# Three of the seven PSUM sums of each down product go to an adding transfer instead of VectorE

## The chip, the cores and the metric

The kernel runs on one core of a Trainium2 chip. Its time is the device time of one launch in microseconds (us), and runs are compared by their medians. Beside the timed runs there is one profiled execution, whose trace gives all durations below.

## The reference

A two-layer decoder trunk in float32 on x of 1024 tokens by 1024 features. Layer 0 is latent attention (low-rank queries and keys/values, rotary keys) and a SwiGLU feed-forward; layer 1 is differential attention over keys and values made from layer 0's result, and again a feed-forward. What the change touches is the second half of the feed-forward, the product with `w_down` and the residual:

```python
D_FF = 2816
def _swiglu(h, w_gate_up, w_down):
    gu = h @ w_gate_up
    return (jax.nn.silu(gu[..., :D_FF]) * gu[..., D_FF:]) @ w_down
...
    h = h + _swiglu(_rmsnorm(h, ffn_norm[l]), ffn_w_gate_up[l], ffn_w_down[l])
return _rmsnorm(h, final_norm)
```

## The kernel before, in words

Everything is stored transposed: features on the 128 partitions, 512 tokens (half a sequence) in a row of a tile. Each float32 operand is split into a high and a low part; a product is three matmuls (high by high, high by low, low by high). ScalarE makes the high part by a copy, VectorE or GpSimd the low part by a subtraction. So a weight `wr` becomes `wh` and `wl`, and an activation `stg` becomes `xh` and `xl`.

The feed-forward of a layer is `block_tail`. Its down product is done by Strassen's scheme in Winograd's form: 2 by 2 blocks, seven products instead of eight. The 2816 inner features are 22 tiles of 128, paired into 11; the pairs are worked off in four groups of 2, 3, 3 and 3 (`GROUPS`). For the first three groups and each of four output blocks n = 0..3, `down(g, n, xs)` runs products 0 to 6. A product has three matmuls for each pair of its group, so 6 matmuls in the first group and 9 in the next two. The last group is done by `down_last`, which the change leaves alone.

The seven products of a block gather in three PSUM banks: `a` (products 0, 2, 4, 6, on top of each other), `b` (product 1) and `c` (products 3 and 5). After each product the bank as it then stands is added into one of four state tiles `h11, h12, h21, h22` in SBUF, which hold the residual and all groups' sums. Before the change each of these seven adds is `add(t, ps)`, a VectorE tensor_tensor that reads the bank and the state tile and writes the state tile. A product that goes on in the same bank has to wait until the bank has been read: product 5 for the sum of product 3, product 6 for the sum of product 4. `h22` gets the sums of products 3 and 4, `h12` of 2 and 5, `h11` of 0 and 1, `h21` of 6.

Beside this, VectorE makes the block differences of the weights (`wr<-wr`), their low parts (`wl`), the sums of the activations of the next group (`stg<-stg`), and part of their low parts (`xl`); GpSimd does the other `xl`. Weights come by SP's DMA queue into eight buffers `wr`, made by `raw()`.

The order of instructions is not that of the code. `Plan` records all operations of a stage, gives each a cost (`cost`: duration on its engine, and delay until another engine can use the result), and replays them by a list schedule: on each engine the operation that can start first. It also decides which buffer a tile gets. The engines then run their queues in that order, so a wait at the head of a queue holds up all behind it. In the trace every operation has line 287, that of the replay, and is told apart by its tiles.

Of the kernel before, what the change touches and what calls it, by code (L numbers as in the profile page):

```python
# [14 lines left out]
AF = mybir.ActivationFunctionType  # L15
ALU = mybir.AluOpType
# [176 lines left out]
class Plan:  # L193
# [100 lines left out]
    def cost(self, engine, name, n, dtype, psum, accum, size):  # L294

        if engine == "tensor":
            if name == "transpose":
                return 0.107, self.HOP
            return n * (1 if dtype == F32R else 6 if n <= 64 else 8) / 2400, self.HOP
        if engine == "scalar":  # L300
            return (0.05 if psum else 0.09) + n / 1200 + 0.19 * accum, self.HOP
        if engine == "vector":
            return 0.067 + n / 960 + 0.063 * (name == "scalar_tensor_tensor" and not psum), self.HOP
        if engine == "gpsimd":
            return (0.245 + n / 1200 if name == "tensor_scalar" else 0.15 + n / 475), self.HOP
        return max(0.45, size / 360e3), 2.2
# [64 lines left out]
def trunk(ctx: ExitStack, tc: tile.TileContext, A: dict):  # L371
    nc = Plan(tc)
# [28 lines left out]
    def bank(name="ps"):  # L401
        if nc.on:
            return nc.ask(banks[0], [P, HF], F32, name, banks[1].get(name))
        return mm.tile([P, HF], F32, name=name, tag="mm")
# [137 lines left out]
    with tc.using_default_side("right"):  # L542
# [9 lines left out]
                t=("z6", "z7", "z8", "z9", "t", "t"), xh=[q + "h" for q in spare], xl=[q + "l" for q in spare],  # L552
# [76 lines left out]
    for k in range(KT):  # L629
        xt[k] = load_x(0, k)  # L630
        raw = wa_p.tile([P, NA * P], F32, name="war", tag="war", bufs=3)
# [434 lines left out]
    def block_tail(layer, half, resid, last, side_work=None, ahead=None, meanwhile=None):  # L1066
# [17 lines left out]
        def htile(n, f, name="h"):  # L1084
            return hp.tile([P, HF], F32, name=name, tag=f"h{n}{f}")
# [11 lines left out]
        def raw(src=None, np_=4):  # L1097
            t = wp.tile([P, HF], F32, name="wr", tag="wr", bufs=8)
            if src is not None:
                nc.sync.dma_start(out=t[:, : np_ * P], in_=src)  # L1100
            return t

        def acc_a():
            return mm2.tile([P, HF], F32, name="pa", tag="pa")

        def acc_c(name="pc"):
            return mm2.tile([P, HF], F32, name=name, tag="pc", bufs=2)
# [90 lines left out]
        def product(ps, i, cols, xs, start=True):  # L1198
            wh, wl = cols.get(i)
            n = len(xs[i])  # L1200
            for k, (xh, xl) in enumerate(xs[i]):
                c = slice(k * P, (k + 1) * P)
                nc.tensor.matmul(ps, lhsT=wh[:, c], rhs=xh, start=start and k == 0, stop=False, skip_group_check=not start)
                nc.tensor.matmul(ps, lhsT=wh[:, c], rhs=xl, start=False, stop=False, skip_group_check=not start)
                nc.tensor.matmul(ps, lhsT=wl[:, c], rhs=xh, start=False, stop=k == n - 1, skip_group_check=not start)
# [127 lines left out]
        def wd(g, n, *how):  # L1333
            p0, np_ = GROUPS[g][0], len(GROUPS[g])
            return Columns([A["wd"][layer, n, :, b, p0 : p0 + np_, :].rearrange("p k c -> p (k c)") for b in range(4)], np_, *how)

        def add(t, ps):
            nc.vector.tensor_tensor(t, t, ps, ALU.add)

        def down(g, n, xs):  # L1340

            cols = wd(g, n)
            if g == 0:
                for f in range(2):
                    for m in (n, n + 4):
                        h[f][m] = htile(m, f)
                        nc.sync.dma_start(out=h[f][m], in_=h_mid[f, m])
            h11, h12, h21, h22 = h[0][n], h[0][n + 4], h[1][n], h[1][n + 4]
            a = acc_a()
            product(a, 0, cols, xs)  # L1350
            add(h11, a)
            yield
            b = bank("pb")
            product(b, 1, cols, xs)
            add(h11, b)
            yield
            product(a, 2, cols, xs, start=False)
            add(h12, a)
            yield
            c = acc_c()  # L1360
            product(c, 3, cols, xs)
            add(h22, c)
            yield
            product(a, 4, cols, xs, start=False)
            add(h22, a)
            yield
            product(c, 5, cols, xs, start=False)
            add(h12, c)
            yield
            product(a, 6, cols, xs, start=False)  # L1370
            add(h21, a)
            yield
# [137 lines left out]
        for i, src in ((5, h[0][4:]), (6, h[1][4:])):  # L1510
            for k in range(4):
                x[i][k] = xtile(i, k)
                c = L if k < 2 else slice(0, HF)
# [31 lines left out]
        for g in range(len(GROUPS) - 1):  # L1545
            after = [[] for _ in range(7)]
            taken = [SLOTS[p] for p in GROUPS[g]]
            free = [p for p in GROUPS[g + 1] if SLOTS[p] not in taken]
            more = [p for p in GROUPS[g + 1] if p not in free]
            side = prepare(after, free, more)  # L1550
            for n in range(4):
                i = 0
                for _ in down(g, n, xs):
                    next(side, None)
                    if n == 3:
                        for p in more:
                            place(after, p, i)
                    i += 1
            xs = after
# [101 lines left out]
    def last0(f, h, r, tmp, _=None):  # L1661
# [18 lines left out]
        low()  # L1680

    block_tail(0, half0, A["x"], last0, positions_and_lambda, ahead0, lambda: both(0)).close()


# [162 lines left out]
    def last1(f, h, r, tmp, c=slice(0, HF)):  # L1847
        for k in range(KT):
# [3 lines left out]
            yield  # L1852

    block_tail(1, half1, h_spill, last1).close()


# [58 lines left out]
```

## Time and profile before

| what | us |
|---|---|
| median of 3 timed runs | 2554.65 (2553.1 to 2556.36) |
| the profiled execution, whole | 2557.78 |
| its span, first to last instruction | 2555.9 |
| mean granted TensorE clock | 0.973 |

The busy time of the engines over the span is PE 2350.6 us, VectorE (DVE) 1992.9, ScalarE (ACT) 1167.8 and GpSimd (POOL) 1063.3. The first three groups of the down product run from about 1010 to 1172 us in layer 0 and from about 2308 to 2470 us in layer 1. A share over the whole span says little about these two stretches; the windows further down are cut there.

### The profile page before, as it was taken

How to read it: one execution, taken by the hardware profiler on the slowest of the kernel's cores; microseconds unless marked ns; L12 is line 12 of the kernel's file. 1: busy time of each engine (PE TensorE's matmuls, PEld its weight loads, DVE VectorE, ACT ScalarE, POOL GpSimd, SP SyncE). 2: the span in 40 equal slices, each digit the busy share in tenths (PEclk: the TensorE clock that was granted, in tenths of full speed). 3: DMA queues.
4: the chain of work that ended last, by engine and by line, in shares of the span. 5: the costliest groups of instructions: out<-in, count | busy, mean ns of one | idle time of the engine just before them, and what ended most of it. 6: DMA issues, size and time to landing. Idle time of an engine off the chain costs nothing. (4 is left out here: it accounts for less than half of the span.)

```text
span 2555.9 us, 37477 instructions
## 1 busy us (share of the span) xinstructions
PE 2350.6 (92%) x12744; PEld 2001.0 (78%) x12744; DVE 1992.9 (78%) x3743; ACT 1167.8 (46%) x2319; POOL 1063.3 (42%) x921
## 2 busy tenths in 40 slices
PE   8699999978899998899999999999879999988997
PEld 6579988757688886777788898888657888876777
DVE  6475555399987879999767667675799887889997
ACT  4145545245344445344345555453444444454442
POOL 2132222176555554123344445443467555543212
PEclk9899999999999999999999999999899999999999
DMA  5132234622322225332233323463612222235322
GB/s 180 21 128 63 67 109 146 179 72 85 116 79 83 85 81 186 105 105 91 76 109 105 110 90 115 140 217 104 185 42 86 89 83 75 91 113 168 108 72 73
DMA packets 162351, 270.29 MB, mean 106 GB/s; under 512 B 22128, under 2 KB 55152, under 8 KB 162160
## 3 DMA queue, kind: packets, MB, share of 16 engines
q1 hardware_dynamic: 162160, 267.90, 34.2%
q8 instruction: 101, 1.65, 0.3%
q14 instruction: 90, 0.74, 0.1%
HBM read 197.43 MB, written 61.49 MB: 101 GB/s over the span
## 5 line engine op out<-in xcount | busy, mean ns | idle before, releaser
L287 ACT ACTIVATE wh<-wr 128x512 fp32r<-128x512 f32 (+2 forms) x588 | 322.2, 557 | 489.1 <-PE pb L287 128.0
L287 DVE TENSOR_TENSOR wl<-wr,wh 128x512 fp32r<-128x512 f32 (+2 forms) x588 | 451.8, 782 | 41.9 <-ACT wh L287 39.7
L287 PE MATMUL pa<-xh,wh 128*128 128x512 f32 (+1 forms) x850 | 342.1, 403 | 38.7 <-DVE h L287 15.9
L287 PE MATMUL pa<-xh,wl 128*128 128x512 f32 (+1 forms) x850 | 339.2, 400 | 19.2 <-DVE wl L287 18.5
L287 PE MATMUL pa<-xl,wh 128*128 128x512 f32 (+1 forms) x850 | 338.7, 399 | 7.1 <-DVE xl L287 7.1
L287 POOL TENSOR_TENSOR wr<-wr 128x512 f32<-128x512 f32 x176 | 250.2, 1426 | 207.2 <-DMA wr<-wgu 99.3
L287 PE MATMUL pb<-xh,wh 128*128 128x256 f32 (+1 forms) x976 | 293.8, 304 | 25.5 <-DVE s L287 19.7
L287 PE MATMUL pb<-xh,wl 128*128 128x256 f32 (+1 forms) x976 | 291.6, 301 | 2.4 <-DVE wl L287 2.2
L287 PE MATMUL pb<-xl,wh 128*128 128x256 f32 (+1 forms) x976 | 292.4, 301 | 1.5 <-DVE xl L287 1.5
L287 POOL TENSOR_TENSOR xl<-stg,xh 128x512 fp32r<-128x512 f32 x66 | 111.0, 1700 | 303.4 <-ACT xh L287 162.9
L287 PEld LDWEIGHTS pa<-xh,wh 128*128 128x128 f32 x850 | 163.1, 192 | 83.4 <-DVE h L287 15.8
L287 PEld LDWEIGHTS pb<-xh,wh 128*128 128x128 f32 x976 | 186.5, 192 | 51.8 <-DVE s L287 30.2
L287 POOL TENSOR_SCALAR p<-p,tot 128x640 f32<-128x640 f32 (+7 forms) x128 | 98.3, 769 | 272.9 <-DVE tot L287 194.7
L287 PEld LDWEIGHTS pa<-xh,wl 128*128 128x128 f32 x850 | 163.8, 193 | 59.9 <-DVE wl L287 28.5
L287 PEld LDWEIGHTS pb<-xl,wh 128*128 128x128 f32 x976 | 187.6, 192 | 15.1 <-DVE xl L287 2.3
L287 PEld LDWEIGHTS pb<-xh,wl 128*128 128x128 f32 x976 | 187.1, 192 | 10.1 <-DVE wl L287 4.4
L287 PEld LDWEIGHTS pa<-xl,wh 128*128 128x128 f32 x850 | 164.2, 193 | 38.7 <-DVE xl L287 9.4
L287 ACT ACTIVATE p<-sc,nmax 128x128 f32<-128x128 f32 (+7 forms) x192 | 141.9, 741 | 78.7 <-DVE nmax L287 53.4
L287 PE MATMUL pc<-xl,wh 128*128 128x512 f32 x352 | 139.8, 397 | 9.9 <-DVE xl L287 9.9
L287 POOL TENSOR_TENSOR qt<-wr 128x256 f32<-128x256 f32 x120 | 105.8, 901 | 98.4 <-DVE wl L287 80.6
L287 PE MATMUL pc<-xh,wh 128*128 128x512 f32 x352 | 138.7, 396 | 8.6 <-DVE h L287 7.8
L287 PE MATMUL pc<-xh,wl 128*128 128x512 f32 x352 | 139.3, 396 | 1.6 <-DVE wl L287 1.6
(288 smaller groups left out, 6310.7 us busy)
## 6 DMA issues: line engine op xcount, KB each, us to landing
wr<-wgu SPq DMA_DIRECT2D x176, 256.0 KB, 3.2
act_d<-s SPq DMA_DIRECT2D x88, 256.0 KB, 2.5
stg<-act_d SPq DMA_DIRECT2D x88, 256.0 KB, 2.8
wr<-wd SPq DMA_DIRECT2D x96, 192.0 KB, 2.4
wr<-wo SPq DMA_DIRECT2D x56, 256.0 KB, 3.9
h<-h_mid SPq DMA_DIRECT2D x48, 256.0 KB, 4.5
h_mid<-h SPq DMA_DIRECT2D x32, 256.0 KB, 2.2
oh<-o_hi SPq DMA_DIRECT2D x28, 256.0 KB, 5.1
```

Of the source, the lines that this page charges most:

```text
L287: return getattr(getattr(self.nc, engine), name)(*map(put, args), **{k: put(a) for k, a in kw.items()})
```

## The change

A new helper `pour(t, ps)` takes the place of `add` for products 1, 3 and 5 of `down`: ScalarE copies the bank into a `wr` buffer, and a DMA issued by GpSimd adds that buffer into the state tile (`accum_op=ALU.add`). The sums of products 0, 2, 4 and 6 stay on VectorE. With three groups, four blocks and three sums that is 36 pours in a layer and 72 in all. `Plan.cost` learns a cost for such a DMA, which only the schedule uses.

```diff
@@ cost
         if engine == "vector":
             return 0.067 + n / 960 + 0.063 * (name == "scalar_tensor_tensor" and not psum), self.HOP
+        if name == "dma_start" and engine == "gpsimd":
+            return 1.2, 3.0
         if engine == "gpsimd":
@@ block_tail
         def add(t, ps):
             nc.vector.tensor_tensor(t, t, ps, ALU.add)
 
+        def pour(t, ps):
+
+            e = raw()
+            nc.scalar.activation(e, ps, AF.Copy)
+            nc.gpsimd.dma_start(out=t, in_=e, accum_op=ALU.add)
+
@@ down
             product(b, 1, cols, xs)
-            add(h11, b)
+            pour(h11, b)
             yield
             product(a, 2, cols, xs, start=False)
             add(h12, a)
             yield
             c = acc_c()
             product(c, 3, cols, xs)
-            add(h22, c)
+            pour(h22, c)
             yield
             product(a, 4, cols, xs, start=False)
             add(h22, a)
             yield
             product(c, 5, cols, xs, start=False)
-            add(h12, c)
+            pour(h12, c)
             yield
             product(a, 6, cols, xs, start=False)
             add(h21, a)
```

The schedule is worked out anew with these costs. VectorE's queue is 72 instructions shorter, ScalarE's and GpSimd's 72 longer each; PE and SP have as many as before, in another order within the two down stages.

First place: VectorE's queue in the third block of the second group (layer 0). Before, from the sum of product 3 (`h_10217<-h_10217,pc_11126`) to those of product 4 (into the same `h_10217`) and 5; the brackets say on which engines or DMA semaphores an instruction waits.

```order
L287 TENSOR_TENSOR h_10217<-h_10217,pc_11126 128x512 [waits PE_49]
L287 TENSOR_TENSOR wl_11163<-wr_11141,wh_11149 128x384 [waits Activation_49]
L287 TENSOR_TENSOR wl_11169<-wr_11073,wh_11157 128x384 [waits Activation_49]
L287 TENSOR_TENSOR h_10353<-h_10353,pa_10992 128x512 [waits PE_49]
L287 TENSOR_TENSOR wr_11141<-wr_11106,wr_11141 128x384 [waits DVE_49]
L287 TENSOR_TENSOR wl_11184<-wr_11075,wh_11161 128x384 [waits Activation_49]
L287 TENSOR_TENSOR xl_11190<-stg_10661,xh_11177 128x512 [waits Activation_49]
L287 TENSOR_TENSOR wr_11197<-wr_11171,wr_11118 128x384 [waits DMAHW7_49,DMAHW5_49,DVE_49]
L287 TENSOR_TENSOR wl_11201<-wr_11141,wh_11192 128x384 [waits Activation_49]
L287 TENSOR_TENSOR wr_11141<-wr_11036,wr_11141 128x384 [waits DVE_49]
L287 TENSOR_TENSOR h_10217<-h_10217,pa_10992 128x512 [waits PE_49]
L287 TENSOR_TENSOR h_10353<-h_10353,pc_11126 128x512 [waits PE_49]
```

The same block after the change, on VectorE: from the sum of product 2 (`h_10345`) to that of product 4 (`h_10213`) and on to the next block's product 0 (`h_10225`).

```order
L287 TENSOR_TENSOR h_10345<-h_10345,pa_11113 128x512 [waits PE_49]
L287 TENSOR_TENSOR wl_11202<-wr_11155,wh_11196 128x384 [waits Activation_49]
L287 TENSOR_TENSOR wr_11155<-wr_11110,wr_11155 128x384 [waits DVE_49]
L287 TENSOR_TENSOR wl_11215<-wr_11151,wh_11206 128x384 [waits PE_49,Activation_49]
L287 TENSOR_TENSOR wl_11233<-wr_11157,wh_11227 128x384 [waits PE_49,Activation_49]
L287 TENSOR_TENSOR wl_11251<-wr_11155,wh_11241 128x384 [waits PE_49,Activation_49]
L287 TENSOR_TENSOR wr_11258<-wr_11256,wr_11217 128x384 [waits DMAHW7_49,DMAHW5_49,DVE_49]
L287 TENSOR_TENSOR h_10213<-h_10213,pa_11113 128x512 [waits DMASW3_49]
L287 TENSOR_TENSOR h_10225<-h_10225,pa_11238 128x512 [waits PE_49]
L287 TENSOR_TENSOR xl_11277<-stg_10695,xh_11249 128x512 [waits Activation_49]
```

The sums out of bank `pc` are gone from VectorE, and the sum of product 4 now waits for a software DMA semaphore (DMASW), that of the pour of product 3.

Second place: PE's queue at the end of the same block. Before, product 6 of the block (`pa_10992`) comes after eight matmuls of the next block (`pa_11165`).

```order
L287 MATMUL pc_11126<-xl_10800,wh_11053 128x512
L287 MATMUL pc_11126<-xh_10783,wl_11090 128x512
L287 MATMUL pa_11165<-xh_10105,wh_11083 128x512
L287 MATMUL pa_11165<-xl_10143,wh_11083 128x512
L287 MATMUL pa_11165<-xh_10105,wl_11116 128x512
L287 MATMUL pa_11165<-xh_10636,wh_11083 128x512
L287 MATMUL pa_11165<-xl_10653,wh_11083 128x512
L287 MATMUL pa_11165<-xh_10636,wl_11116 128x512
L287 MATMUL pa_10992<-xh_10310,wh_11157 128x512 [waits DVE_49,Activation_49]
L287 MATMUL pa_10992<-xl_10328,wh_11157 128x512
```

After, it (`pa_11113`) comes after product 0 of the next block (`pa_11238`) and seven matmuls of its product 1 (`pb_11263`).

```order
L287 MATMUL pa_11238<-xl_10681,wh_11128 128x512
L287 MATMUL pa_11238<-xh_10665,wl_11145 128x512
L287 MATMUL pb_11263<-xh_10230,wh_11167 128x512
L287 MATMUL pb_11263<-xl_10367,wh_11167 128x512
L287 MATMUL pb_11263<-xh_10230,wl_11178 128x512
L287 MATMUL pb_11263<-xh_10135,wh_11167 128x512
L287 MATMUL pb_11263<-xl_10283,wh_11167 128x512
L287 MATMUL pb_11263<-xh_10135,wl_11178 128x512
L287 MATMUL pb_11263<-xh_10715,wh_11167 128x512
L287 MATMUL pa_11113<-xh_10305,wh_11139 128x512 [waits DVE_49]
L287 MATMUL pa_11113<-xl_10320,wh_11139 128x512
```

In this block product 3 is followed by products 4 and 5, nine matmuls each, and by these sixteen: 34 matmuls stand between the end of product 3 and the start of product 6.

Third place: GpSimd's queue at the start of layer 0's down stage. Before, it held only low-part subtractions here; now DMA issues stand between them.

```order
-L287 TENSOR_TENSOR xl_10369<-stg_10346,xh_10360 128x512 [waits Activation_49,Pool_49]
-L287 TENSOR_TENSOR xl_10382<-stg_10320,xh_10371 128x512 [waits DMAHW1_49,Activation_49]
-L287 TENSOR_TENSOR xl_10394<-stg_10198,xh_10375 128x512 [waits Activation_49]
-L287 TENSOR_TENSOR xl_10462<-stg_10436,xh_10448 128x512 [waits Activation_49]
+L287 DMA h_10288<-wr_10347 128x512 [waits DMAHW5_49,DVE_49,Activation_49]
+L287 TENSOR_TENSOR xl_10374<-stg_10329,xh_10351 128x512 [waits Activation_49,Pool_49]
+L287 TENSOR_TENSOR xl_10391<-stg_10194,xh_10364 128x512 [waits DVE_49,Activation_49]
+L287 DMA h_10336<-wr_10314 128x512 [waits DMAHW4_49,DVE_49]
+L287 TENSOR_TENSOR xl_10415<-stg_10316,xh_10387 128x512 [waits DMAHW7_49,Activation_49]
+L287 TENSOR_TENSOR xl_10449<-stg_10422,xh_10437 128x512 [waits Activation_49]
+L287 DMA h_10302<-wr_10447 128x512 [waits DMAHW1_49,DVE_49,Activation_49]
```

A pour whose turn comes while GpSimd is in a subtraction, or whose predecessor in the queue still waits, is issued later.

## Rows read from the trace of the kernel before

**Rows 1.** Page: busy us of each engine, share of the span, instructions.

```profile
PE 2350.6 (92%) x12744; PEld 2001.0 (78%) x12744; DVE 1992.9 (78%) x3743; ACT 1167.8 (46%) x2319; POOL 1063.3 (42%) x921
```

**Rows 2.** Windows of both down stages: length, busy us and count by engine.

```profile
core 0: us, PE busy (x) PEld busy (x) DVE busy (x) ACT busy (x) POOL busy (x), PEclk, DMA share, GB/s
1010.00:1065.00 55.00, 44.27 (x177) 33.25 (x178) 55.00 (x98) 23.72 (x50) 17.19 (x11) 0.97 0.46 146
...
1108.00:1135.00 27.00, 22.95 (x98) 17.79 (x97) 26.82 (x36) 13.62 (x26) 15.15 (x9) 1.00 0.42 128
...
2308.00:2362.00 54.00, 44.26 (x177) 33.29 (x177) 54.00 (x96) 22.81 (x48) 16.75 (x11) 0.97 0.45 142
2362.00:2405.00 43.00, 42.93 (x181) 35.13 (x182) 41.28 (x79) 14.71 (x29) 0.00 (x0) 0.96 0.36 111
2405.00:2432.00 27.00, 22.99 (x98) 17.77 (x98) 26.82 (x37) 13.57 (x27) 15.18 (x9) 1.00 0.43 128
2432.00:2470.00 38.00, 38.00 (x168) 31.31 (x168) 35.48 (x65) 14.11 (x28) 2.43 (x2) 1.00 0.21 62
```

**Rows 3.** Chain that ended last, around 2362 us: start, us, what.

```profile
2361.54 0.48 DVE wl L287
2362.07 3.16 PE pa L287 x7
...
2367.37 2.05 PE pa L287 x9
```

**Rows 4.** PE's waits, 2308 to 2363: total us, times, longest.

```profile
PE pa L287 <- DVE wl L287: 3.8, 2, 3.2
PE pc L287 <- DVE h L287: 3.1, 1, 3.1
PE pa L287 <- DVE h L287: 2.2, 2, 1.6
PE pc L287 <- DVE wl L287: 0.8, 1, 0.8
PE pa L287 <- ACT wh L287: 0.7, 1, 0.7
```

**Rows 5.** PE's waits, 2405 to 2432.

```profile
PE pa L287 <- DVE h L287: 2.6, 2, 1.4
PE pa L287 <- ACT wh L287: 1.4, 1, 1.4
```

**Rows 6.** VectorE's sums from banks c, b, 2308 to 2362: busy, mean ns.

```profile
L287 DVE TENSOR_TENSOR h<-h,pc 128x512 f32<-128x512 f32 x9 | 6.0, 673 | 0.0
L287 DVE TENSOR_TENSOR h<-h,pb 128x512 f32<-128x512 f32 x5 | 3.4, 672 | 0.0
```

**Rows 7.** The same, 2405 to 2432.

```profile
L287 DVE TENSOR_TENSOR h<-h,pc 128x512 f32<-128x512 f32 x3 | 2.0, 675 | 0.0
L287 DVE TENSOR_TENSOR h<-h,pb 128x512 f32<-128x512 f32 x1 | 0.7, 671 | 0.0
```

**Rows 8.** VectorE's timeline from 1112 us: start, us, instruction.

```profile
1112.16 0.68 DVE L287 TENSOR_TENSOR h<-h,pc 128x512 f32<-128x512 f32 x1
1112.76 1.41 DVE L287 TENSOR_TENSOR xl<-stg,xh 128x512 fp32r<-128x512 f32 x1
1114.09 1.65 DVE L287 TENSOR_TENSOR wl<-wr,wh 128x384 fp32r<-128x384 f32 x1
1115.66 0.67 DVE L287 TENSOR_TENSOR h<-h,pa 128x512 f32<-128x512 f32 x1
```

**Rows 9.** GpSimd's timeline at the same place.

```profile
1112.33 3.00 POOL L287 TENSOR_TENSOR xl<-stg,xh 128x512 fp32r<-128x512 f32 x2 [1.24 <-ACT xh L287]
```

**Rows 10.** ScalarE's copies out of a bank, whole span: busy, mean ns.

```profile
L287 ACT ACTIVATE s<-pa 128x512 f32<-128x512 f32 x88 | 51.5, 585 | 12.3 <-PE pa L287 12.1
```

**Rows 11.** Page, DMA issues: size, median us from issue to landing.

```profile
act_d<-s SPq DMA_DIRECT2D x88, 256.0 KB, 2.5
...
h<-h_mid SPq DMA_DIRECT2D x48, 256.0 KB, 4.5
```

## The prediction

> **What bounds the kernel now.** I read the busy shares first, then cut windows through the two stages that the change touches, then asked who waits for whom there, and followed the chain of waits. Over the span PE is the busiest engine (92%) and VectorE has 78% [rows 1], which would say that VectorE's work is free. The windows say otherwise [rows 2]. In layer 1 the first three groups fall into four stretches: from 2308 to 2362 us VectorE is busy for 54.00 of 54 us and PE for only 44.26; from 2362 to 2405 PE for 42.93 of 43; from 2405 to 2432 VectorE for 26.82 of 27 and PE for 22.99; from 2432 to 2470 PE for all 38. Layer 0 shows the same two VectorE stretches, 1010 to 1065 (55.00 of 55) and 1108 to 1135 (26.82 of 27). In the VectorE stretches GpSimd is busy too (16.75 and 15.18 us), in the others hardly. The chain of waits changes hands where the windows do: it runs through VectorE until 2362 and through PE from there [rows 3]. PE's own waits are the time that can be won: in the first stretch 3.8 + 3.1 + 2.2 + 0.8 + 0.7 = 10.6 us, nearly all for VectorE [rows 4], in the third 2.6 + 1.4 = 4.0 us [rows 5]. So VectorE is the bound in two stretches per layer, PE in the other two, and a sum taken off VectorE is worth something in the first kind only.
>
> **The change part by part.** *Sums removed from VectorE.* All sums from banks c and b before the last group are poured. In the first stretch these are 9 + 5 = 14 [rows 6], in the third 3 + 1 = 4 [rows 7]. Each is busy for 0.67 us, but the next instruction starts 0.60 us after it (1112.16 to 1112.76 [rows 8]), so one is worth 0.60. That gives 14 x 0.60 = 8.4 us and 4 x 0.60 = 2.4 us, both below what PE waits there (10.6 and 4.0), so PE can take up all of it: 10.8 us per layer, 21.6 in both. The other 18 sums of a layer lie in PE's stretches or behind them, and I count them at nothing: PE's work covers them.
>
> *Copies on ScalarE.* 36 per layer of 0.585 us [rows 10]. ScalarE is busy for 22.81 of 54 and 13.57 of 27 us [rows 2], so 14 x 0.585 = 8.2 us and 4 x 0.585 = 2.3 us fit, and I cost them at nothing. Without this cover each would delay a `wh` that PE needs, at 0.585 apiece. The bank is even free sooner: product 5 no longer waits for VectorE to read bank c, which today is PE's single wait of 3.1 us [rows 4].
>
> *The transfers.* No row shows a DMA issued by GpSimd, nor one that adds. For GpSimd's part the bounds are 0 (an issue by SP is not even counted as work) and 1.5 us, half of the pair of subtractions [rows 9]; I take 1.5, its only row. From issue to landing, 256 KB take 2.5 us out of SBUF and 4.5 into the state tiles [rows 11]; this one also reads its destination, so I take 3.5, the middle. A pour is then 0.585 + 1.5 + 3.5 = 5.6 us after its product; from 0.585 + 0 + 2.5 = 3.1 to 0.585 + 1.5 + 4.5 + 3.0 = 9.6 when GpSimd has just begun a pair of subtractions (3.00 us [rows 9]).
>
> The Trainium skill (DMA: Bandwidth & Descriptors, "Anatomy of one DMA") fits a transfer from GpSimd at about 2.0 us plus its bytes at 436 GB/s, which is an estimate of 2.6 us here, issue and landing together; by it no pour would be late and the sum would stay at the full 21.6. No run here shows it for an adding transfer.
>
> *The wait that is added.* VectorE's sum of product 4 goes into the same `h22` as the pour of product 3, and now waits for it; behind it on VectorE's queue stand the low parts of the next block's weights, and behind those PE; and product 6 waits for it directly. The queue on PE leaves 34 matmuls between product 3 and product 6, at 2.05 / 9 = 0.228 us each [rows 3] 7.7 us; less the sum itself (0.67) a pour may take 7.1 us. At 5.6 it is in time. Behind a pair of subtractions it is at 5.6 + 3.0 = 8.6 and 1.5 us late. Five blocks of the first stretch and two of the third are at risk, and GpSimd is busy there for 31% and 56% of the time: about 0.31 x 5 + 0.56 x 2 = 2.7 late blocks, 4.0 us; since VectorE can now be ahead by what it was relieved of, I take 3 us per layer, 6 in both (from 0 to 24 blocks x 2.5 = 60).
>
> *The rest.* The pours hold `wr` buffers, so some weight loads on SP's queue now wait for a pour instead of for VectorE, and ScalarE's copy into a reused buffer too; with a landing of 3.5 us I cost this at nothing, and it belongs to the case of late pours. The weights' and activations' arithmetic is the same.
>
> **The sum.** 21.6 - 6 = 15.6 us. The profiled execution took 2557.78 us, of which 2555.9 are the span: 2557.8 - 15.6 = 2542.2. The median of the timed runs is 3.1 us below the profiled one, so I predict 2539 us.
>
> **Rivals.** *All of PE's waits go.* With VectorE no longer the bound, PE's 10.6 + 4.0 = 14.6 us per layer vanish, 29.2 in all. PE also runs slowly after a long wait: seven matmuls take 3.16 us after the one at 2362 [rows 3], 0.45 each against 0.228, half the clock (1.2 against 2.4 GHz), 1.6 us; with the like after the 3.1 us wait some 3.2 per layer. That is 36 us, 2522 profiled, 2519 in the median. For it: the waits are nearly all for VectorE. Against it: 18 sums at 0.60 do not cover 14.6 us, and the bursts in which GpSimd's subtractions slow VectorE's stay.
>
> *Nothing.* The new waits give back what the sums bring, or PE's next wait (for `wh`, 1.4 us [rows 5]) takes over: within 5 us of before, 2555. For it: PE is at its limit in 81 of 162 us per layer.
>
> *Late pours (slower).* The place is VectorE's sum of product 4; the price is each microsecond over 7.1, because a wait at the head of VectorE's queue holds up the `wl` behind it. It decides from 21.6 / 24 blocks = 0.9 us, a pour of 8.0 us on average. If the 14 blocks in VectorE's stretches have a pour of 9.6, that is 14 x 2.5 = 35 us, less 21.6: 13 us slower, 2568 in the median. For it: GpSimd is busy in just those stretches, and its queue is in order. Against it: the 5.6 that I take lies well below.
>
> *Descriptor work blocks VectorE (not faster).* While GpSimd subtracts, VectorE's instructions with two SBUF inputs are stretched from about 0.68 to 1.41 us, while its sums out of PSUM stay at 0.67 [rows 8, 9]. If issuing a pour did the same, each would cost 1.41 - 0.68 = 0.73 us: for the 36 pours of VectorE's stretches 26 us against 21.6 gained, 5 us slower, 2560; more where it also uncovers PE's stretches. The Trainium skill (SBUF — State Buffer, "SBUF: two separate sides") says that VectorE and GpSimd share a pair of ports as an exclusive lock, which an instruction of VectorE takes in a two-port mode or, with two SBUF inputs, only against one of GpSimd that reads SBUF; the stretched rows agree with it. The same page warns that GpSimd cannot write descriptors while VectorE is in a two-port mode; VectorE's instructions here have two tensor inputs, so by the page neither blocking would happen, and I lower this case to 0.10.
>
> **How the numbers follow.** Forecast 0.50, with its own range 2530 to 2548 (late blocks from all of the 6 us twice over to none, and some of PE's half-clock time won back). All waits go 0.12, nothing 0.14, late pours 0.14, blocked VectorE 0.10. A measurement of this kernel can tell about 0.2%, 5 us, from no change. Faster: 0.50 + 0.12 = 0.62. Same: 0.14. Slower: 0.14 + 0.10 = 0.24. The range of 8 in 10 reaches from the first rival (2519) past the blocked VectorE to 2562, and leaves out the late pours.
>
> **What would show it.** Right: VectorE's busy time 72 x 0.67 = 48 us lower; PE's waits for `h` in the first stretch of each layer smaller, the one of 3.1 us before product 5 gone; the stretch from 2308 on 8 us shorter, the PE-bound ones as long as now; copies of 0.585 us from pb and pc on ScalarE; few waits of VectorE's `h<-h,pa` for a DMA. Wrong: VectorE idle before `h<-h,pa` with the pour as releaser, by more than about 0.9 us a block; `xl` and `wl` on VectorE stretched while GpSimd issues; or ScalarE and SP waiting for pours to give back `wr`.

## The result, and the profile after

The changed kernel takes 2573.85 us (median of 4 runs, 2571.53 to 2576.22) against 2555.51 for the kernel before in the same session: ratio 1.0073, 95% interval 1.0056 to 1.0091. It is 18 us slower; the forecast was 15.6 us faster. The profiled execution has a span of 2574.4 us.

The page, busy times [rows 1]; the transfers, as GpSimd's work and as DMA issues [rows 11]:

```profile
PE 2364.7 (92%) x12744; PEld 2014.3 (78%) x12744; DVE 1979.0 (77%) x3671; ACT 1202.6 (47%) x2391; POOL 1114.5 (43%) x993
...
L287 POOL DMA_DIRECT2D h<-wr x72 | 62.9, 881 | 214.6 <-ACT wr L287 87.1
...
h<-wr POOLq DMA_DIRECT2D x72, 256.0 KB, 3.7
```

VectorE has 72 instructions less, but only 14 us less to do, not 48. A transfer occupies GpSimd for 0.88 us (I took 1.5) and lands 3.7 us after its issue begins.

Where the time went is seen when the trace is cut at matmuls that stand at the same place of PE's queue in both kernels. The change moves matmuls between the 5014th and the 5694th (layer 0's down stage), the 5694th and the 6153rd (the join to layer 1's attention), and the 11728th and the 12462nd (layer 1's down stage). The down stages go from 182.5 + 192.7 = 375.2 us to 187.9 + 201.0 = 388.9, so +13.7; the join from 98.7 to 104.5, +5.8. The rest differs by 1 us in sum. Windows of the two stages, first of before, then of after, as in [rows 2]:

```profile
1006.00:1189.00 183.00, 164.12 (x684) 129.00 (x683) 178.65 (x298) 76.98 (x152) 47.33 (x30) 0.97 0.37 115
2303.00:2496.00 193.00, 174.57 (x737) 138.02 (x736) 188.58 (x321) 80.68 (x160) 45.48 (x28) 0.98 0.36 112
```

```profile
1003.00:1190.00 187.00, 166.81 (x679) 132.12 (x678) 169.43 (x263) 92.78 (x186) 69.54 (x65) 0.94 0.66 163
2314.00:2515.00 201.00, 181.42 (x736) 143.62 (x736) 181.97 (x286) 97.44 (x195) 68.60 (x64) 0.93 0.61 152
```

VectorE is busy for a smaller part of the time (169 of 187 us, for 179 of 183), and yet PE takes longer, at a lower granted clock (0.94 and 0.93 for 0.97 and 0.98). PE's idle time in the two stages is 41.0 us for 37.3. The waits are for the same engine as before, in longer pieces: 9 of them last over 2 us, 27.2 us in all, for 6 with 17.3. PE's longest sums of waits in layer 0's stage, before:

```profile
PE pa L287 <- DVE h L287: 7.9, 6, 2.4
PE pc L287 <- DVE h L287: 4.0, 2, 3.4
PE pa L287 <- DVE wl L287: 3.8, 2, 3.2
```

and after:

```profile
PE pa L287 <- DVE h L287: 13.6, 5, 4.1
PE pc L287 <- DVE wl L287: 2.8, 2, 2.4
```

After such a wait PE runs at half its clock for a while (1.2 for 2.4 GHz). PE's timeline after the longest wait; the granted clock from 1188 to 1190 us is 0.50:

```profile
1187.12 0.50 PE L287 MATMUL pa<-xh,wh 128*128 128x512 f32 x1 [4.11 <-DVE h L287]
1187.45 0.40 PE L287 MATMUL pa<-xl,wh 128*128 128x512 f32 x1
...
1188.39 0.63 PE L287 MATMUL pa<-xl,wh 128*128 128x512 f32 x1
1188.82 0.63 PE L287 MATMUL pa<-xh,wl 128*128 128x512 f32 x1
1189.25 0.63 PE L287 MATMUL pa<-xh,wh 128*128 128x512 f32 x1
```

The starts from 1188.39 on lie 0.43 us apart, not 0.228. In both stages 121 matmuls start over 0.3 us behind the one before without a wait, for 74 before, and what they lose is 22.9 us for 11.2. Of them 92 and 37 lie in stretches that the profile shows at half the clock (50.5 us of them in the two stages, for 17.1 before); these lose 19.3 us for 7.2. So the 13.7 us are 3.7 of idle time and some 10 to 12 of half clock.

What makes the waits long is VectorE's own work. The timeline of all engines from 1005.4 us, rows of GpSimd, VectorE and PE:

```profile
1005.47 1.03 POOL L287 DMA_DIRECT2D h<-wr  x1 [2.40 <-DVE stg L287]
...
1006.02 3.57 DVE L287 TENSOR_TENSOR stg<-stg 128x512 f32<-128x512 f32 x1
...
1006.25 2.79 POOL L287 TENSOR_TENSOR xl<-stg,xh 128x512 fp32r<-128x512 f32 x2
...
1010.72 0.68 DVE L287 TENSOR_TENSOR h<-h,pa 128x512 f32<-128x512 f32 x1
...
1011.45 0.79 PE L287 MATMUL pa<-xh,wh 128*128 128x512 f32 x1 [3.66 <-DVE h L287]
```

GpSimd issues a transfer and then subtracts twice; a VectorE instruction with two SBUF inputs, 0.68 us alone, lasts 3.57 and ends 0.55 us after both subtractions; the sum behind it comes late and PE waits for it. In the kernel before no such instruction in the two stages lasts over 1.79 us, since VectorE gets its turn between two subtractions (1.41 and 1.65 in [rows 8]). In the changed kernel 19 last over 2 us, at most 4.58, and beside each of the 19 GpSimd has an issue directly ahead of its subtractions, between them or directly behind. I call *stretch* what VectorE's instructions in the two stages take above the shortest one with the same tiles and shapes, where that is over 0.15 us: 43.3 us before, 62.8 after. (The expectations below have 42 and 57 for these two, from a narrower count that compares only instructions with the same waits.)

The join is another matter. PE's timeline there:

```profile
1259.82 0.39 PE L287 MATMUL psp<-ah,wl 128*128 128x512 f32 x1
1267.22 0.44 PE L287 MATMUL sc<-ks,qa 128*128 128x128 f32 x1 [7.01 <-DVE ks L369]
```

The planner, which counts in its own costs, has put a score matmul of attention (`sc`) ahead of the next projections (`psp`); in the kernel before it stands behind 24 of their matmuls. It waits 7.0 us at the head of PE's queue for VectorE's `ks`, which stands behind VectorE's `wr` and `al`; in the kernel before nothing waits there for over 1.1 us.

### The profile page after: what moved, and what is told of

The parts are those of the page before. It is cut to its first block, busy times and chain, and to the rows that moved or that the text cites. A ratio compares the mean times of both kernels' runs of the same rounds, so it can differ in the third digit from the quotient of the medians.

```text
span 2574.4 us, 37666 instructions
## 1 busy us (share of the span) xinstructions
PE 2364.7 (92%) x12744; PEld 2014.3 (78%) x12744; DVE 1979.0 (77%) x3671; ACT 1202.6 (47%) x2391; POOL 1114.5 (43%) x993
## 3 DMA queue, kind: packets, MB, share of 16 engines
q8 instruction: 101, 1.65, 0.3%
## 4 chain that ended last, share of the span: by engine, by line
PE 59%; DVE 26%; DMA 6%; issue 5%; ACT 2%; POOL 2%; SPq 0%; DVEq 0%; ACTq 0%; POOLq 0%
PE pa L287 15%; PE pb L287 9%; PE psp L287 8%; DVE wl L287 6%; PE pc L287 6%; PE sc L287 5%; PE psv L287 4%; PE pso L287 4%; DVE s L287 3%; PE pswo L287 3%; DVE xl L287 3%; DVE h L287 3%; PE tp L287 2%; DVE wr L287 1%; DMA rd<-rsy 1%
## 5 line engine op out<-in xcount | busy, mean ns | idle before, releaser
L287 DVE TENSOR_TENSOR wl<-wr,wh 128x512 fp32r<-128x512 f32 (+2 forms) x588 | 445.0, 771 | 53.1 <-ACT wh L287 51.7
L287 POOL DMA_DIRECT2D h<-wr x72 | 62.9, 881 | 214.6 <-ACT wr L287 87.1
```

Source lines behind the costliest of these rows:

```text
L287: return getattr(getattr(self.nc, engine), name)(*map(put, args), **{k: put(a) for k, a in kw.items()})
```

## The experiments

Three things change at once: sums leave VectorE, transfers come, and the planner makes another order. The theory of the order lays the loss on the last; the port theory on the transfers, whose issue on GpSimd would stretch VectorE's instructions beside GpSimd's subtractions; rivals are the waits for the landed sums, the transfers' bytes, and that the sums were never on the path. The first four runs separate them. Two kernels keep the order of before ("old order"), two that of the changed kernel ("new order"): all operations are recorded and planned as before, and only at the replay is one put in place of another. Stretch and stages are of both layers; "> 2 us" counts VectorE's instructions in them. The ratios are of medians; stages, join and stretch are of one profiled execution each, while timed runs of one kernel differ by up to some 16 us within a session (2547.4 to 2563.5 for the kernel before, beside e13 to e15). So differences of a few us in these columns are not told from chance by one row, and rows of different sessions are better compared by their ratios.

| run | ratio to before (95%) | stages | join | stretch | > 2 us |
|---|---|---|---|---|---|
| before | 1 | 375.2 | 98.7 | 43.3 | 0 |
| after | 1.0073 (1.0056 to 1.0091) | 388.9 | 104.5 | 62.8 | 19 |
| e1 old order, pours | 1.0141 (1.0118 to 1.0164) | 417.5 | 97.5 | 56.1 | 14 |
| e2 old order, copies only | 0.9940 (0.9924 to 0.9956) | 361.0 | 98.0 | 48.3 | 0 |
| e3 new order, VectorE's sums | 1.0091 (1.0076 to 1.0106) | 389.4 | 106.8 | 44.3 | 0 |
| e4 new order, copies only | 0.9997 (0.9986 to 1.0008) | 366.2 | 104.1 | 45.6 | 0 |
| e5 new order, plain transfers by GpSimd | 1.0041 (1.0027 to 1.0054) | 373.8 | 103.1 | 50.4 | 10 |
| e6 new order, plain transfers by ScalarE | 1.0010 (0.9997 to 1.0024) | 369.8 | 103.9 | 46.3 | 0 |
| e7 old order, pours, subtractions on VectorE | 1.0054 (1.0039 to 1.0069) | 392.5 | 96.5 | 3.2 | 1 |
| e8 after + subtractions on VectorE | 0.9873 (0.9857 to 0.9890) | 352.9 | 98.1 | 2.0 | 0 |
| e9 before + 72 idle issues | 1.0031 (1.0017 to 1.0045) | 385.7 | 96.3 | 51.1 | 7 |
| e10 before + subtractions on VectorE | 0.9919 (0.9904 to 0.9933) | 366.0 | 98.4 | 2.0 | 0 |
| e11 as e8, products 1 and 5 | 0.9892 (0.9877 to 0.9907) | 356.6 | 98.8 | 2.4 | 0 |
| e12 as e8, products 1, 3, 5, 6 | 0.9911 (0.9893 to 0.9930) | 363.3 | 99.4 | 2.9 | 1 |
| e13 new order, adding into a dead buffer | 1.0108 (1.0085 to 1.0131) | 392.0 | 104.8 | 55.1 | 12 |
| e14 as e8, copies only | 0.9826 (0.9798 to 0.9854) | 345.1 | 95.6 | 2.6 | 0 |
| e15 after, other costs | 1.0051 (1.0033 to 1.0069) | 382.3 | 107.5 | 57.4 | 15 |

**e1 and e2: the old order.** The record is VectorE's sum; the replay does this instead (e2 without the second line):

```diff
-nc.vector.tensor_tensor(t, t, ps, ALU.add)
+tc.nc.scalar.activation(e, put(ps), AF.Copy)
+tc.nc.gpsimd.dma_start(out=put(t), in_=e, accum_op=ALU.add)
```

> The order that the planner made for the kernel before, kept word for word on TensorE, VectorE and SyncE; in it the 72 sums of products 1, 3 and 5 are replaced, where they stood, by ScalarE's copy and GpSimd's adding transfer, with a buffer that is dead at that place. Order theory (the loss of 18 us comes from the planner's new order: 5.8 us where attention of layer 1 begins, the rest in the two down stages): at or below before, 2540 to 2556. Port theory (the loss comes from the transfers themselves, whose issue puts GpSimd's subtractions back to back against VectorE's two-input operations): 2560 to 2570, with VectorE operations over 2.2 us in the trace again. The prediction's own sum, order left out, is 2539.

> As the run before, but the transfer is left out too: ScalarE copies the bank and nothing adds the copy, so three of seven sums are missing from the result. It is the most that the order of before could give back. If VectorE's sums stand on the path as predicted (21.6 us): 2534. If TensorE's waits in the down stages are of single operations and not of VectorE's load: 2550 to 2556. If the transfers cost something by themselves, this run is faster than the one with them by that.

Measured 2593.4 and 2538.9 us. Without the sums and without transfers the stages are 14.2 us shorter, PE's idle time 26.9 for 37.3 us: this is what the forecast's first step was about, two thirds of its 21.6. The transfers then cost 56.5 us, more than either theory had. In an order that leaves them no room, VectorE waits for landings as well; its waits in layer 1's stage of e1, where the changed kernel has 2.6 us of the kind:

```profile
DVE h L287 <- DMA h<-e: 7.6, 4, 3.7
...
DVE xl L287 <- DMA h<-e: 5.3, 1, 5.3
...
DVE stg L287 <- DMA h<-e: 1.9, 1, 1.9
```

**e3 and e4: the new order.** In e3 the recorded copy is replayed as VectorE's sum and the transfer as nothing; in e4 only the transfer is left out:

```diff
+nc.swap = lambda **kw: None
 nc.gpsimd.dma_start(out=t, in_=e, accum_op=ALU.add)
+nc.swap = None
```

> The new order kept word for word on TensorE and SyncE, but VectorE does the 72 sums again, at the place of ScalarE's copies (four of them, where the state tile is not there yet, at the place of the transfer from the copy), and no transfer is issued. Order theory: no faster than after, 2574 to 2590, since the order is as bad and VectorE has its work back. Port theory: near before plus the 5.8 us at the start of attention, 2558 to 2564.

> The new order word for word, with ScalarE's copies, but without the transfers: three of seven sums are missing from the result. Order theory: as after within a few us, 2568 to 2575. Port theory: the 18 us of stretched operations and what they delay go, 2555 to 2562, and VectorE's two-input operations take at most 1.8 us again.

Measured 2577.4 and 2552.5 us. Both theories are half right, and the stages add up: the new order costs 389.4 - 375.2 = 14.2 us (with VectorE's sums where the copies stand, which is no order that the planner made for them), taking the sums off VectorE brings 389.4 - 366.2 = 23.2, the transfers cost 388.9 - 366.2 = 22.7; in sum 13.7. By the ratios the transfers cost 1.0073 - 0.9997, or 19 us of the whole. The join is 4 to 8 us longer than before in all runs in the new order and in none in the old, so they are the order's. With the transfers the stretch is 62.8 us, without 45.6: 17.2 us more of VectorE's time, beside 22.7 us of the stages. Windows of e4, for those of after above:

```profile
999.00:1178.00 179.00, 163.58 (x682) 129.49 (x683) 162.38 (x264) 93.67 (x188) 44.02 (x30) 0.97 0.38 119
2300.00:2487.00 187.00, 173.57 (x732) 138.86 (x733) 171.25 (x284) 97.86 (x194) 41.85 (x28) 0.97 0.37 115
```

VectorE is busy for 333.6 us with the instructions that take 351.4 beside transfers, and the clock is back at 0.97.

**e5 and e6: plain transfers.** In the new order, each transfer writes the copy to DRAM:

```diff
-nc.gpsimd.dma_start(out=t, in_=e, accum_op=ALU.add)
+tc.nc.gpsimd.dma_start(out=dump[k], in_=put(e))   # e6: tc.nc.scalar
```

> The new order word for word; GpSimd still issues its 72 transfers, but each is a plain one that writes ScalarE's copy to a buffer in DRAM, without adding and without touching the state (three of seven sums are missing). Without any transfer this order took 2552, with the adding ones 2574. Issue theory (what costs is GpSimd's issuing, which delays its subtractions and bunches them against VectorE): 2568 to 2574, VectorE operations over 2.2 us remain. Adding theory (what costs is the sum itself: the wait for the state tile, the wait of the next sum, the bytes read and written back): 2552 to 2558.

> As the run before, but the plain transfers to DRAM are issued by ScalarE behind its copy, not by GpSimd (three of seven sums are missing). The same bytes leave SBUF, and GpSimd issues nothing. Issue theory: 2552 to 2558, unless ScalarE itself is held up by issuing. If the transfers' traffic costs: as much as with GpSimd, 2565 to 2574.

From ScalarE the same bytes cost 3.6 us in the stages (3 us by the ratios to e4, within the noise) and stretch nothing over 2 us. From GpSimd they cost 7.6 (11 by the ratios), with 10 long instructions: the issue counts more than the traffic. But a plain transfer occupies GpSimd for 0.55 us only, and costs a third of an adding one in the stages, some half of it by the ratios (11 of 19 us); e5, at 2560.3 us, lies between the theories.

**e7 and e8: GpSimd does nothing but issue.** e7 is e1 with the subtractions replayed by VectorE; e8 is the changed kernel, planned anew with

```diff
-split(*t, staged[p][i], sub=nc.vector if i in (0, 1, 3, 5) else nc.gpsimd)
+split(*t, staged[p][i])
```

> The order of before, adding transfers where VectorE's sums stood (2593 with GpSimd's subtractions), and now the 66 subtractions of GpSimd in the down stages done by VectorE at the same place of the program, so that GpSimd does nothing there but issue transfers. Port theory (two-input VectorE operations are stretched by GpSimd's subtractions that queue up behind its issues): VectorE gets 66 x 0.6 = 40 us of work and loses 70 to 80 us of stretching and waiting; 2550 to 2565. Landing theory (the wait for landed sums costs): no better than 2585. Work theory (VectorE's load counts alone): 2593 + 40 = 2630 at most.

> The changed kernel, with one edit: the subtractions that GpSimd does in the down stages are given to VectorE before planning, so the planner orders it anew. Port theory: 2574 less the stretching (57 us of VectorE time in the two stages) plus 40 us of work, so faster than after by 5 to 25 us, 2549 to 2569, and perhaps faster than before. Work theory: slower than after, 2580 to 2600.

e7 takes 2563.4 us, 30 less than e1 (22 by the ratios, as the sessions differ) though VectorE has 40 us more to do: port theory. It stays above before; VectorE still waits 13.7 us for landings in layer 1's stage, which fits, but no run in the old order has the moved subtractions without the pours, so this part is argued. e8 takes 2516.8 us, below both kernels and below what I expected. Windows of its stages:

```profile
994.00:1164.00 170.00, 160.63 (x682) 127.32 (x681) 155.34 (x291) 94.23 (x187) 36.18 (x39) 0.99 0.72 182
2270.00:2453.00 183.00, 173.28 (x737) 138.29 (x735) 166.38 (x312) 99.09 (x196) 32.59 (x37) 0.98 0.68 168
```

VectorE does the subtractions too and is busy for 321.7 us, 29.7 less than in the changed kernel, since next to nothing is stretched, with all 72 issues there.

**e9: issues alone.** The kernel before, in its order, with

```diff
 tc.nc.vector.tensor_tensor(put(t), put(t), put(ps), ALU.add)
+tc.nc.gpsimd.dma_start(out=dump[len(poured) % 64], in_=ones)
```

> The kernel before in its own order, with all its sums on VectorE; added are only 72 small plain transfers that GpSimd issues where the three sums stand (32 KB of ones to DRAM, nobody waits for them). Port theory (an issue ahead of a subtraction on GpSimd lets VectorE's two-input operation wait until GpSimd's queue is empty): slower than before by 5 to 25 us, with VectorE operations of 2.2 us and more in the trace. Adding theory (the cost lies in the adding transfers' bytes and landings): 0 to 2 us.

7 us slower, 10.5 in the stages, and no sum, copy or wait of the old order is touched. VectorE's timeline, then GpSimd's:

```profile
2435.14 2.57 DVE L287 TENSOR_TENSOR stg<-stg 128x512 f32<-128x512 f32 x1
2437.63 0.68 DVE L287 TENSOR_TENSOR xl<-stg,xh 128x512 fp32r<-128x512 f32 x1
```

```profile
2434.59 2.55 POOL L287 TENSOR_TENSOR xl<-stg,xh 128x512 fp32r<-128x512 f32 x2
2437.08 1.09 POOL L1367 DMA_DIRECT2D dump<-ones  x2
```

Here the issues come behind the pair of subtractions, and VectorE gets no turn until both subtractions are through.

**e10 to e12: what e8 owes to which part.** e10 is the kernel before with e8's edit; e11 and e12 pour other products:

```diff
-            pour(h22, c)      # e11
+            add(h22, c)
...
-            add(h21, a)       # e12
+            pour(h21, a)
```

> The kernel before, with the subtractions of the down stages moved from GpSimd to VectorE before planning, and no pours: the control for the run of 2517 us that had both. If GpSimd's subtractions take from VectorE by stretching about what they save it (42 us of stretching against 40 us of work): 2545 to 2560. If the gain of that run were the moved subtractions alone: 2517 to 2525.

> Pours of products 1 and 5 only, subtractions on VectorE. By VectorE's load: 24 sums go back to it, 24 x 0.6 = 14 us more than in the run of 2517, so 2525 to 2531. If the wait of product 4's sum for product 3's landing costs more than its work: 2505 to 2515.

> Pours of products 1, 3, 5 and 6, subtractions on VectorE. By VectorE's load 24 sums fewer than in the run of 2517, but TensorE waits only 19 us in all in its two down stages: 2508 to 2517. If 96 issues and landings get in each other's way, or ScalarE's copy comes too late for TensorE's next bank: 2518 to 2530.

e10 takes 2538.3 us, ratio 0.9919, between its two ranges: GpSimd's subtractions were a loss by themselves. Only 9.2 us of it lie in the stages. Just ahead of them, where the first group's operands are made (from the 4801st matmul to the 5014th and from the 11601st to the 11728th), the kernel before takes 74.2 us and e10 63.5, since PE waits less for VectorE's `s`; layer 0, before, then e10:

```profile
PE pb L287 <- DVE s L287: 7.3, 3, 6.1
```

```profile
PE pb L287 <- DVE s L287: 3.4, 3, 2.2
```

e8 has this gain too (63.3 us). Against e8's 0.9873 the pours are worth another half per cent once GpSimd does not subtract, 366.0 - 352.9 = 13.1 us in the stages. With before and after this makes a square of timed kernels, each in an order of its own: beside GpSimd's subtractions the pours cost 0.7% (1.0073), without them they bring 0.5% (0.9873 against 0.9919). Pours of 1 and 5 alone, and of four products, are 3.7 and 10.4 us behind e8 in the stages; by the ratios the first is not told from e8, and the second is slower, and slower than either range expected.

**e13 and e14: what is left in a transfer.** e13 is e5 with `accum_op=ALU.add`; e14 is e8 with e4's edit.

> The new order word for word; the 72 transfers from GpSimd's queue add, but into a buffer in DRAM that nothing else uses, so no sum waits for them and they wait for no state tile (three of seven sums are missing from the result). Issue theory: the issue is as long as in the changed kernel (0.88 us) and the time is as after, ratio 1.007 to 1.010 to before. Wait theory (the state's waits are the 14 us): as with plain transfers, 1.003 to 1.005.

> The order of the run of 2517 us word for word (pours, and the subtractions of the down stages on VectorE), but the transfers are left out, and with them three of seven sums. Port theory: the transfers cost next to nothing once GpSimd subtracts nothing there: 0 to 5 us faster than that run, ratio 0.985 to 0.988 to before. If the transfers cost about 20 us by themselves, as they did in the new order beside the subtractions: 0.979 or less.

e13 is no faster than the changed kernel although no state tile is waited for, but it doesn't settle the question: these transfers land after 5.0 us, and `wr` buffers come back late; SP's waits in layer 1's stage:

```profile
SPq L287 <- DVE wl L287: 36.1, 15, 6.6
SPq L287 <- DMA dump<-wr: 33.7, 10, 5.8
```

In e14 the stages are 7.8 us shorter than in e8: a third of the 22.7 us that the same transfers cost beside the subtractions. The ratios are less clear: 0.9873 - 0.9826 is 12 us, 8 either way, for the 19, 5 either way, of after against e4, and e14's ratio lies between the two that were expected. That the transfers cost less without subtractions rests on the stages and on the square above.

**e15: the planner's numbers.**

```diff
-            return 1.2, 3.0
+            return 0.88, 3.3
```

> The changed kernel with the planner told what the trace shows of the transfer: 0.88 us of issue and 3.3 us until the sum is there, for 1.2 and 3.0. If the 14 us of the new order come of wrong numbers, it loses them: ratio 0.999 to 1.003. If they are a draw of the planner, another draw: 1.000 to 1.012, and whether TensorE waits 7 us at the start of attention of layer 1 is decided anew. The transfers' own cost stays in either case.

Another draw: the stages 6.6 us shorter than in the changed kernel, the join 3.0 longer. Truer costs don't take the loss at the join away; how much of the 6.6 us is order, no run tells.

## Why the prediction was wrong

- *VectorE bounds the two stretches, and sums taken off it are won.* Right in kind. e2, in the order that I had read, gains 14.2 us for the 21.6; e8 against e10, 13.1. PE's waits shrank but did not go.
- *Copies on ScalarE hidden.* Nearly: in the changed kernel PE waits 0.9 and 1.3 us for them in the two stages.
- *A pour takes 5.6 us, new waits 6 us.* Near enough. From the issue's start to the landing it is 3.7, after a copy of 0.59, so 4.3 where GpSimd is free; the estimate of 2.6 that the prediction sets beside its sum is 1.1 short of the 3.7, and right for e5's plain transfers (2.7). VectorE's waits for landings are small where the planner has made room, 3.7 us in the two stages.
- *The weights' buffers at nothing.* Not quite: SP waits 48.5 us for pours over the span, but its waits in the stages go from 296 to 308 us only.
- **The step that failed is the price of the transfers.** The sum has 6 us for them, all for late landings, and nothing for what GpSimd's issues do to VectorE; in the stages they cost 22.7 us (e4 against after), of which plain transfers by GpSimd make 7.6 (e5); small idle ones cost 10.5 in the old order (e9). I had the place as a rival (descriptor work blocks VectorE) and gave it 0.10, at 0.73 us a pour, 26 us for those in VectorE's stretches. That 26 is near 22.7 is luck: not the issue stretches an instruction by 0.73, but the run of subtractions next to it, by up to 4. I lowered the rival by the Trainium skill (SBUF — State Buffer, "SBUF: two separate sides"), by which an issue and an instruction with two tensor inputs don't block each other (the Trainium skill calls the reason inferred). For issues alone the traces agree: e8 has 72 and a stretch of 2.0 us. But I applied the rule to the issue by itself; here the issue stands next to subtractions that read SBUF, and both long rows shown lie over such subtractions. For those the Trainium skill (SBUF — State Buffer, "Summary: rules for kernel authors") says that of an instruction with two SBUF inputs and a GpSimd operation that reads SBUF, the one issued second is blocked until the first is done. The kernel before agrees (1.79 us at most, one subtraction's wait); next to an issue the wait went over up to three of them.
- **And a term was missing: the order.** I worked with the order of before, in which only the pours' own instructions move. The planner's new order costs 14.2 us in the stages and 8.1 at the join (e3).
- *The sign.* For the stages 21.6 - 6 was forecast; measured in the stages, 23.2 - 22.7 - 14.2 = -13.7. Of the signs that I had named, `xl` stretched beside GpSimd's issues was the one that came; VectorE idle for the pours was not.
- *Half clock.* I had it in a rival only, as a gain. It made 10 to 12 of the 13.7 us: longer waits cost more than their length.

What stays open: how much of an adding transfer's price over a plain one (15 us in the stages of the new order, some 8 by the ratios) is its longer issue and how much the later return of buffers, and why GpSimd's subtractions leave VectorE no turn when an issue stands next to them.

## What to carry to other kernels

Before work is moved to a third engine, look at what that engine already does beside the one to be relieved: here the pours made the kernel 0.7% slower next to GpSimd's subtractions and 0.5% faster without them, and moving the subtractions to the busy VectorE (0.8%) was worth more than the change was forecast to bring. With a planner, the order is a term of the sum: replaying the old order with the new operations, and the new order with the old ones, takes it apart in four runs. And read a stretched instruction by its length against the shortest of its form; a busy share counts it as work.

## What the runs showed of the hardware

- Next to a GpSimd issue, VectorE's instructions with two SBUF inputs lasted up to 4.58 us over GpSimd's subtractions (after), and 5.69 over two multiplications and two subtractions (e9), for 1.80 at most in the runs without issues (before, e2, e3, e4, e6); 72 issues without subtractions left a stretch of 2.0 us in all (e8). Sums out of PSUM differed among themselves by 0.02 us at most (before, after, e9).
- A plain transfer of 256 KB to DRAM occupies GpSimd for 0.54 us in the median, one of 32 KB too (e5, e9), and one that adds 256 KB into SBUF for 0.87 (after); issued by ScalarE, plain transfers left the stretch at 46.3 us for 45.6 without (e6, e4).
- GpSimd's 66 subtractions of 128 x 512 (1.62 us each in the median, before) saved VectorE 66 x 0.60 = 40 us, and the stretch beside them cost it 43.3 in the stages alone.
